# Attention's sums of values written feature-major, with the values as weights

## The chip, the cores and the metric

One Trainium2 chip, one core of it. The metric is device microseconds of one execution of the whole program. The core has five engines that run side by side: TensorE (PE, with its weight loads shown as PEld), VectorE (DVE), ScalarE (ACT), GpSimd (POOL) and SyncE (SP). All data transfers of the parts that matter here are issued from SP's queue, in order.

## What is computed

Two layers of a hybrid trunk over 1024 latent tokens and 256 context tokens. The token mixer of each layer has a Hyena long convolution, an mLSTM and an attention; the part that changes is the attention. It has 6 query heads in two groups of 3, one key/value head for each group, head size 64. A latent token sees the keys within 128 positions, all 256 context keys and a sink:

```python
s_loc = where(mask, einsum(q, k_window) * scale, -1e30)
s_ctx = einsum(q, k_ctx) * scale
p = softmax(concatenate([s_loc, s_ctx, s_sink]))
out = einsum(p_window, v_window) + einsum(p_ctx, v_ctx)
```

A context token sees the context keys and the sink alone. In the second layer only latent tokens are asked for. The concatenated heads go through one output projection.

## The kernel before

Everything is tiled to 128 rows. The program is written as Python generators, one for each stream of work, and `weave` takes steps from them in given proportions; a planner with a simulated timeline then sets the order of instructions on each engine, and each engine runs its own list in order.

`mix_heads` has two stages of interest in each layer. In the first, the projections (`project_o`, `attention_inputs` of both groups), the mLSTM and `attend` of group 0 are woven together. In the second, two halves of the Hyena convolution (`hyena`, with `dft4` on VectorE), the mLSTM and `attend` of group 1 are. After it `mixed` loads the heads' outputs back (`mixed_parts`) and runs the output projection.

`attention_inputs` normalises and rotates queries and keys, two token tiles at a time, transposes them, and puts the queries through the tile `qst` (one buffer) to the DRAM tensor `qd` with one store for two token tiles (L522).

`attend` runs over blocks of 128 queries: 10 blocks for each group in layer 0, 8 in layer 1, so 36 in all. `nk` is the number of 128-key tiles of a block: 5 for six of the eight latent blocks, 4 for the two at the ends, 2 for the two context blocks. For each of three heads:

- scores by matmuls in fp32r into the PSUM bank "s" (two buffers, L552 and L558), moved by VectorE into `S` (two buffers) with the running minimum, then exponentials with their sum on ScalarE (L561);
- `nk` transposes of `S` on TensorE into the bank "t" (L566; the fifth goes to a part of `po`, L570), copied by ScalarE into `PT` (two buffers, L567 and L571);
- `nk` matmuls in f32 that sum the values into `po`, the transposed weights being the stationary operand and 64 columns of `va` the moving one (L573):

```python
for i, kb in enumerate(kbs):
    nc.tensor.matmul(out=po[:, h * HD:(h + 1) * HD], lhsT=PT[:, i * P:(i + 1) * P], rhs=va[:, kb, :],
                     start=(i == 0), stop=(i == nk - 1))
```

After the third head the sums' reciprocals `es` are made. Here queries lie on the partitions, so three ScalarE instructions scale the heads (L148), two transposes turn the result (L585, L586), two ScalarE copies take it out of PSUM to `aev` (L589, L590), and two stores of 128 and of 64 partitions put it into the DRAM tensor `mixa` (L591, L592), laid out as 128 x 3 x tokens.

`split` (L136, L141) makes the fp32r halves of what `mixed_parts` loads (L1151).

Of the kernel before, what the change touches and what calls it, by code (L numbers as in the profile page):

```python
# [46 lines left out]
ON_PE = False  # L47
TK, TV, FW = (3, 2), (8, 7), (6, 1)
UW = 5, 3, 18
PT2 = 1  # L50
SC = (1, 0, 0, 1)
SB = ("f0", "f1"), ("t", "o")
WE, ML = (10, 10), (8, 8)
# [29 lines left out]
class Kernel:  # L83
# [388 lines left out]
    def attention_inputs(self, l, g, D, ap, ai):  # L472

        nc, A, d = self.nc, self.A, self.L[l]
        last = l == DEPTH - 1
        kt = self.t(ap, [P, T], F32R, "kk")
        va = self.t(ap, [P, NT, HD], F32, "va")
        qd = self.dram([P, 3, T], f"qd{g}")
        self.att[g] = (qd, kt, va)
        w = self.wgroup(l, f"g{g}")  # L480
        for t0 in (8, 6, 4, 2, 0):
            n = self.t(ai, [P, 2, 4, HD], F32, "n", bufs=2)
            for i in range(2):
                ps = self.tok_tile(w, t0 + i, 320)
                nc.scalar.activation(out=n[:, i], in_=ps[:, :256].rearrange("p (h d) -> p h d", h=4), func=AF.Copy)
                nc.scalar.activation(out=va[:, t0 + i, :], in_=ps[:, 256:320], func=AF.Copy)
                yield
            n3 = n.rearrange("p t h d -> p (t h) d")
            t1 = self.t(ai, [P, 8, HD], F32, "t1")
            nc.scalar.activation(out=t1, in_=n3, func=AF.Square)  # L490
            ss = self.t(ai, [P, 8], F32, "ss", bufs=2)
            nc.vector.tensor_reduce(out=ss, in_=t1, axis=AX.X, op=ALU.add)
            r = self.rsqrt(ai, ss, 1.0 / HD, [P, 8], "ar", 1)
            nc.vector.tensor_tensor(out=n3, in0=n3, in1=r.unsqueeze(2).to_broadcast([P, 8, HD]), op=ALU.mult)
            nc.gpsimd.tensor_tensor(out=n[:, :, 0:3], in0=n[:, :, 0:3], in1=d["qkw"][:, 0:1].unsqueeze(1).to_broadcast([P, 2, 3, HD]), op=ALU.mult)
            nc.gpsimd.tensor_tensor(out=n[:, :, 3], in0=n[:, :, 3], in1=d["qkw"][:, 1:2].to_broadcast([P, 2, HD]), op=ALU.mult)
            if t0 < 8:
                rt = self.t(ai, [P, 2, 2, HD], F32, "rt")
                nc.sync.dma_start(out=rt, in_=A["rope"][:, t0:t0 + 2])
                t2 = self.t(ai, [P, 8, HD], F32, "t1")  # L500
                for i in range(2):
                    t5 = t2[:, 4 * i:4 * i + 4].rearrange("p h (a b i) -> p h a b i", a=2, b=2)
                    n5 = n[:, i].rearrange("p h (a b i) -> p h a b i", a=2, b=2)
                    s5 = rt[:, i, 1, :].rearrange("p (a b i) -> p a b i", a=2, b=2)
                    for b in range(2):
                        nc.vector.tensor_tensor(out=t5[:, :, :, b, :], in0=n5[:, :, :, 1 - b, :],
                                                in1=s5[:, :, b, :].unsqueeze(1).to_broadcast([P, 4, 2, 16]), op=ALU.mult)
                    nc.gpsimd.tensor_tensor(out=n[:, i], in0=n[:, i], in1=rt[:, i, 0:1, :].to_broadcast([P, 4, HD]), op=ALU.mult)
                nc.vector.tensor_tensor(out=n3, in0=n3, in1=t2, op=ALU.add)
            hl = self.t(ai, [P, 2, 4, 2, HD], F32R, "hl")  # L510
            hf = hl.bitcast(F32)
            nc.scalar.activation(out=hl[:, :, :, 0, :], in_=n, func=AF.Copy)
            nc.vector.tensor_tensor(out=hl[:, :, :, 1, :], in0=n, in1=hf[:, :, :, 0, :], op=ALU.subtract)
            qst = self.t(ai, [P, 3, 2, P], F32, "qst")
            for i in range(2):
                tt = t0 + i
                pq = self.ps("f1")
                for h in range(4):
                    nc.tensor.transpose(pq[:, h * P:(h + 1) * P], hf[:, i, h].rearrange("p b d -> p (b d)"), self.ident)
                nc.scalar.activation(out=qst[:, :, i, :], in_=pq[:, :384].rearrange("p (h c) -> p h c", h=3), func=AF.Copy)  # L520
                nc.vector.tensor_copy(out=kt[:, tt * P:(tt + 1) * P], in_=pq[:, 384:])
            nc.sync.dma_start(out=qd[:, :, t0 * P:(t0 + 2) * P], in_=qst.rearrange("p h t c -> p h (t c)"))  # L522
            yield

    def attend(self, l, g, mix, ap):
        nc, d = self.nc, self.L[l]
        qd, kt, va = self.att[g]
        for nb in ORDER if l < DEPTH - 1 else ORDER[2:]:
# [8 lines left out]
            for i in range(2):  # L537
                for b in range(2):
                    nc.sync.dma_start(out=qf[b * HD:(b + 1) * HD, i], in_=qd[i * HD:(i + 1) * HD, :, nb * P:(nb + 1) * P])
            att = self.t(ap, [P, 3, HD], F32, "att", bufs=1)  # L540
            m3 = self.t(ap, [P, 3], F32, "m3", bufs=2)
            s3 = self.t(ap, [P, 3], F32, "s3", bufs=2)
            po = self.ps("o")
            for h in range(3):
# [14 lines left out]
                nc.vector.tensor_tensor_reduce(out=S[:, w:w + 256], in0=p2[:, :256], in1=self.amask[:, 384:640], scale=-0.125,  # L559
                                               scalar=init, op0=ALU.add, op1=ALU.min, accum_out=m3[:, h:h + 1])  # L560
                nc.scalar.activation(out=S[:, :w + 256], in_=S[:, :w + 256], func=AF.Exp, scale=-1.0, bias=m3[:, h:h + 1], accum_out=s3[:, h:h + 1])  # L561
                PT = self.t(ap, [P, 640], F32, "PT", bufs=2)
                pt1 = self.ps("t")
                n1 = min(nk, 4)
                for i in range(n1):
                    nc.tensor.transpose(pt1[:, i * P:(i + 1) * P], S[:, i * P:(i + 1) * P], self.ident)  # L566
                nc.scalar.activation(out=PT[:, :n1 * P], in_=pt1[:, :n1 * P], func=AF.Copy)  # L567
                if nk > 4:
                    pt2 = po[:, (2 + h % 2) * P:(3 + h % 2) * P]
                    nc.tensor.transpose(pt2, S[:, 4 * P:5 * P], self.ident)  # L570
                    (nc.scalar.copy if PT2 else nc.vector.tensor_copy)(out=PT[:, 4 * P:5 * P], in_=pt2)  # L571
                for i, kb in enumerate(kbs):
                    nc.tensor.matmul(out=po[:, h * HD:(h + 1) * HD], lhsT=PT[:, i * P:(i + 1) * P], rhs=va[:, kb, :],  # L573
                                     start=(i == 0), stop=(i == nk - 1))
                yield
            es = self.t(ap, [P, 3], F32, "es", bufs=2)
            nc.vector.tensor_tensor(out=es, in0=d["sink"][:, g * 3:g * 3 + 3], in1=m3, op=ALU.add)
            nc.scalar.activation(out=es, in_=es, func=AF.Exp)
            nc.vector.tensor_tensor(out=es, in0=es, in1=s3, op=ALU.add)
            nc.vector.reciprocal(out=es, in_=es)  # L580
            self.scale(att, po[:, :192].rearrange("p (h e) -> p h e", h=3), es, SC[0])
            af = att.rearrange("p h e -> p (h e)")
            pt = po[:, 2 * P:]
            big, small = (0, 128) if g == 0 else (64, 0)
            nc.tensor.transpose(pt[:, :P], af[:, big:big + P], self.ident)  # L585
            nc.tensor.transpose(pt[0:HD, P:2 * P], af[:, small:small + HD], self.ident)  # L586
            ev = self.t(ap, [P, 2, P], F32, "aev", bufs=1)
            cs = slice(nb * P, (nb + 1) * P)
            nc.scalar.activation(out=ev[:, 0, :], in_=pt[:, :P], func=AF.Copy)  # L589
            nc.scalar.activation(out=ev[0:HD, 1, :], in_=pt[0:HD, P:2 * P], func=AF.Copy)  # L590
            nc.sync.dma_start(out=mix["att"][:, 2 * g, cs], in_=ev[:, 0, :])  # L591
            nc.sync.dma_start(out=mix["att"][g * HD:(g + 1) * HD, 1, cs], in_=ev[0:HD, 1, :])  # L592
            yield


# [536 lines left out]
    def mixed_parts(self, mix, c, ops, late, room=()):  # L1132

        nc, (c0, n) = self.nc, c
        s = slice(c0, c0 + n)
        for ks in ((0, 1), (2,), (3, 4), (5,), (6, 7)) if late else ((0, 1), (2,), (6, 7), (3, 4), (5,)):
            if not room:
                raws = self.t(self.wp, [P, 1024], F32, "raw", 2)
            for i, k in enumerate(ks):
                raw = room[k].bitcast(F32)[:, :n] if room else raws[:, i * 512:i * 512 + n]  # L1140
                hi, lo = ops[k]
                if 3 <= k < 6:

                    R, b0 = (2, SEQ) if c0 >= SEQ else (8, 0)
                    j0, nj = (c0 - b0) // R, n // R
                    src = mix["hy"][:, k - 3, b0:b0 + P * R].rearrange("p (r j) -> p r j", r=R)[:, :, j0:j0 + nj]
                    ins = nc.sync.dma_start(out=raw.rearrange("p (r j) -> p r j", r=R), in_=src)
                    raw = raw.rearrange("p (r j) -> p j r", r=R)
                    hi, lo = (t.rearrange("p (j r) -> p j r", r=R) for t in (hi, lo))
                else:  # L1150
                    ins = nc.sync.dma_start(out=raw, in_=mix["att"][:, k, s] if k < 3 else mix["ml"][:, k - 6, s])  # L1151
                if "m" in TOK:
                    self.tc.stamp_issue_order_token(ins.ins, "loads")
                self.split(hi, lo, raw)
            yield
# [230 lines left out]
    def run(self):  # L1386
        with ExitStack() as st:
# [7 lines left out]
            hg = self.start()  # L1395
            xd = self.A["xin"]
            for l in range(DEPTH):
                mix = {"att": self.dram([P, 3, T], "mixa"), "hy": self.dram([P, 3, T], "mixh"), "ml": self.dram([P, 2, T], "mixm")}
                D = self.D
                self.project(l, D)  # L1400
                self.mix_heads(l, D, mix, hg)
# [430 lines left out]
```

## Time and profile before

| | us |
|---|---|
| median of 3 runs | 3440.06 |
| lowest and highest | 3439.55, 3443.77 |
| the profiled execution's own time | 3429.16 |
| its span, first to last instruction | 3427.4 |
| TensorE busy in it | 3195.6 (93%) |
| mean granted TensorE clock | 0.959 |

The profile is of one execution, which was faster than the median by 10.9 us; 1.8 us of its own time lie around the span. A row of a group gives busy time in all, mean time of one instruction in ns, and the engine's idle time ahead of the group with what ended it. A matmul's end is modelled, and matmuls overlap, so the time that one takes of the engine is read from the starts of its neighbours in the order of time, not from its mean. An f32 matmul that isn't a transpose shows as two records.

### The profile page before, as it was taken

How to read it: one execution, taken by the hardware profiler on the slowest of the kernel's cores; microseconds unless marked ns; L12 is line 12 of the kernel's file. 1: busy time of each engine (PE TensorE's matmuls, PEld its weight loads, DVE VectorE, ACT ScalarE, POOL GpSimd, SP SyncE). 2: the span in 40 equal slices, each digit the busy share in tenths (PEclk: the TensorE clock that was granted, in tenths of full speed). 3: DMA queues.
4: the chain of work that ended last, by engine and by line, in shares of the span. 5: the costliest groups of instructions: out<-in, count | busy, mean ns of one | idle time of the engine just before them, and what ended most of it. 6: DMA issues, size and time to landing. Idle time of an engine off the chain costs nothing. (4 is left out here: it accounts for less than half of the span.)

```text
span 3427.4 us, 48440 instructions
## 1 busy us (share of the span) xinstructions
PE 3195.6 (93%) x17486; PEld 2748.8 (80%) x17486; DVE 2072.1 (60%) x3673; ACT 1378.1 (40%) x2941; POOL 1071.9 (31%) x944
## 2 busy tenths in 40 slices
PE   7988999999979999997989999999889699999998
PEld 3966798888858888886867897899888478887787
DVE  8669667796494444344565755556885854444443
ACT  5544456444362223223451543456344533333210
POOL 2355333111142333334881230133112444433000
PEclk8999999999989999999999999999899899999999
DMA  6556545543611212126662364445336222223432
GB/s 236 194 196 210 172 138 170 142 120 91 185 57 59 74 68 74 59 74 237 227 230 87 118 203 152 148 134 179 102 90 194 68 74 80 80 83 104 157 98 74
DMA packets 336926, 449.09 MB, mean 131 GB/s; under 512 B 46576, under 2 KB 249124, under 8 KB 334895
## 3 DMA queue, kind: packets, MB, share of 16 engines
q1 hardware_dynamic: 336312, 445.67, 40.3%
q8 instruction: 138, 2.26, 0.3%
q14 instruction: 101, 0.83, 0.1%
q10 hardware_dynamic: 375, 0.34, 0.0%
HBM read 329.73 MB, written 116.16 MB: 130 GB/s over the span
## 5 line engine op out<-in xcount | busy, mean ns | idle before, releaser
L136 ACT ACTIVATE w<-raw 128x512 fp32r<-128x512 f32 (+3 forms) x286 | 221.1, 800 | 470.4 <-PE f L169 130.6
L168 PE MATMUL f<-b,w 128*128 128x512 f32 (+1 forms) x912 | 339.0, 383 | 49.2 <-ACT b L136 41.3
L141 DVE TENSOR_TENSOR w<-raw,w 128x512 fp32r<-128x512 f32 (+3 forms) x266 | 274.1, 1046 | 149.4 <-ACT w L136 141.5
L141 DVE TENSOR_TENSOR w<-S,w 128x512 fp32r<-128x512 f32 x168 | 145.7, 888 | 342.9 <-ACT w L136 322.7
L169 PE MATMUL f<-b,w 128*128 128x512 f32 (+1 forms) x912 | 334.8, 368 | 2.4 <-DVE b L141 2.4
L170 PE MATMUL f<-b,w 128*128 128x512 f32 (+1 forms) x912 | 333.3, 366 | 0.0
L168 PE MATMUL mm<-w,hh 128*128 128x256 f32 (+2 forms) x928 | 279.4, 302 | 8.3 <-ACT hh L326 5.4
L254 POOL TENSOR_TENSOR mraw<-mraw,silb 128x1024 f32<-128x1024 f32 x96 | 248.3, 2592 | 105.7 <-DVE mod L263 65.2
L170 PE MATMUL mm<-w,hl 128*128 128x256 f32 (+2 forms) x928 | 276.3, 300 | 4.8 <-DVE hl L327 4.8
L169 PE MATMUL mm<-w,hh 128*128 128x256 f32 (+2 forms) x928 | 278.1, 300 | 0.0
L1373 DVE SCALAR_TENSOR_TENSOR x<-f,mod,x 128x512 f32<-128x512 f32 (+1 forms) x256 | 166.3, 663 | 154.3 <-PE f L170 149.4
L168 PEld LDWEIGHTS f<-b,w 128*128 128x128 f32 x912 | 179.0, 199 | 86.5 <-ACT b L136 45.4
L169 PEld LDWEIGHTS f<-b,w 128*128 128x128 f32 x912 | 176.4, 193 | 32.4 <-DVE b L141 4.6
L170 PEld LDWEIGHTS f<-b,w 128*128 128x128 f32 x912 | 176.0, 193 | 26.9
L136 ACT ACTIVATE w<-S 128x512 fp32r<-128x512 f32 x168 | 101.0, 625 | 219.9 <-POOL S L1178 201.4
L168 PEld LDWEIGHTS mm<-w,hh 128*128 128x128 f32 x928 | 178.3, 192 | 12.9 <-ACT hh L326 7.4
L170 PEld LDWEIGHTS mm<-w,hl 128*128 128x128 f32 x928 | 177.4, 192 | 6.4 <-DVE hl L327 6.0
L169 PEld LDWEIGHTS mm<-w,hh 128*128 128x128 f32 x928 | 178.5, 192 | 0.8 <-DVE w L141 0.3
L271 ACT ACTIVATE mraw<-mraw 128x1024 f32<-128x1024 f32 x96 | 101.6, 1059 | 145.4 <-POOL mraw L254 145.4
L1240 PE MATMUL a<-hb,w 128*128 128x512 f32 x352 | 139.6, 397 | 7.9 <-DVE hb L141 7.8
L1240 PE MATMUL b<-hb,w 128*128 128x512 f32 x352 | 138.7, 394 | 8.2 <-DVE hb L141 8.0
L1239 PE MATMUL d<-hb,w 128*128 128x512 f32 x352 | 141.2, 401 | 4.5 <-ACT w L136 4.5
(678 smaller groups left out, 8893.3 us busy)
## 6 DMA issues: line engine op xcount, KB each, us to landing
mraw<-in_wmodT SPq DMA_DIRECT2D x96, 512.0 KB
raw<-in_wgu SPq DMA_DIRECT2D x88, 512.0 KB
act<-g SPq DMA_DIRECT2D x88, 256.0 KB
raw<-in_wdn SPq DMA_DIRECT2D x44, 512.0 KB
raw<-act SPq DMA_DIRECT2D x42, 512.0 KB
raw<-in_wout SPq DMA_DIRECT2D x32, 512.0 KB
q<-qd SPq DMA_DIRECT2D x144, 96.0 KB
eoL<-eo SPq DMA_DIRECT2D x64, 192.0 KB
```

The costliest lines, as they stand in the source:

```text
L136: ins = nc.scalar.activation(out=hi, in_=src, func=AF.Copy)
L141: (eng or nc.vector).tensor_tensor(out=lo, in0=src, in1=hi.bitcast(F32), op=ALU.subtract)
L168: nc.tensor.matmul(out=ps, lhsT=ah, rhs=bh, start=(i == 0), stop=False, skip_group_check=on)
L169: nc.tensor.matmul(out=ps, lhsT=ah, rhs=bl, start=False, stop=False, skip_group_check=on)
L170: nc.tensor.matmul(out=ps, lhsT=al, rhs=bh, start=False, stop=(i % part == part - 1 or i == n - 1), skip_group_check=on)
L254: nc.gpsimd.tensor_tensor(out=raw, in0=raw, in1=sil[v], op=ALU.mult)
L271: self.nc.scalar.activation(out=raw, in_=raw, func=AF.Copy, accum_out=o)
L1239: nc.tensor.matmul(out=ps, lhsT=ah[:, ks], rhs=bh, start=start and k == 0, stop=False, skip_group_check=not start)
L1240: nc.tensor.matmul(out=ps, lhsT=ah[:, ks], rhs=bl, start=False, stop=False, skip_group_check=not start)
L1373: nc.vector.scalar_tensor_tensor(out=x, in0=ps[:, :n], scalar=d["mod"][:, 40 + m, v:v + 1], in1=x, op0=ALU.mult, op1=ALU.add)
```

## The change

Values become the weights. For each key tile one matmul with `va[:, kb, :]` (128 x 64) as the stationary operand streams the transposed weights of all three heads, 384 columns, into `po[0:64]`; the result has features on partitions and queries along the row. `PT` becomes one tile for a whole block, 5 x 3 x 128 columns, with one buffer. The reciprocals, which lie on the query partitions, are spread over 64 partitions by a matmul of ones with `R`, three scaled identities side by side (made by ScalarE in a buffer of `S`), into a buffer of "s"; ScalarE copies the spread factors to `ev`, which lies in the last fifth of `PT`, and VectorE multiplies `po` by them. The scaling on L148, the two transposes and the two copies are gone. One store puts the 64 x 3 x 128 result into `mixa`, now laid out as 64 x 6 x tokens, and `mixed_parts` reads a 128-row tile of it with two loads of 64 partitions. `qst` holds one token tile, with a store for each.

```diff
-            qst = self.t(ai, [P, 3, 2, P], F32, "qst")
             for i in range(2):
                 tt = t0 + i
                 pq = self.ps("f1")
                 for h in range(4):
                     nc.tensor.transpose(pq[:, h * P:(h + 1) * P], hf[:, i, h].rearrange("p b d -> p (b d)"), self.ident)
-                nc.scalar.activation(out=qst[:, :, i, :], in_=pq[:, :384].rearrange("p (h c) -> p h c", h=3), func=AF.Copy)
+                qst = self.t(ai, [P, 3, P], F32, "qst")
+                nc.scalar.activation(out=qst, in_=pq[:, :384].rearrange("p (h c) -> p h c", h=3), func=AF.Copy)
                 nc.vector.tensor_copy(out=kt[:, tt * P:(tt + 1) * P], in_=pq[:, 384:])
-            nc.sync.dma_start(out=qd[:, :, t0 * P:(t0 + 2) * P], in_=qst.rearrange("p h t c -> p h (t c)"))
+                nc.sync.dma_start(out=qd[:, :, tt * P:(tt + 1) * P], in_=qst)
...
-            att = self.t(ap, [P, 3, HD], F32, "att", bufs=1)
+            PT = self.t(ap, [P, 5, 3, P], F32, "PT", bufs=1)
...
-                PT = self.t(ap, [P, 640], F32, "PT", bufs=2)
...
-                nc.scalar.activation(out=PT[:, :n1 * P], in_=pt1[:, :n1 * P], func=AF.Copy)
+                nc.scalar.activation(out=PT[:, :n1, h, :], in_=pt1[:, :n1 * P].rearrange("p (k c) -> p k c", k=n1), func=AF.Copy)
                 if nk > 4:
-                    pt2 = po[:, (2 + h % 2) * P:(3 + h % 2) * P]
-                    nc.tensor.transpose(pt2, S[:, 4 * P:5 * P], self.ident)
-                    (nc.scalar.copy if PT2 else nc.vector.tensor_copy)(out=PT[:, 4 * P:5 * P], in_=pt2)
-                for i, kb in enumerate(kbs):
-                    nc.tensor.matmul(out=po[:, h * HD:(h + 1) * HD], lhsT=PT[:, i * P:(i + 1) * P], rhs=va[:, kb, :],
-                                     start=(i == 0), stop=(i == nk - 1))
+                    nc.tensor.transpose(po[:, 3 * P:], S[:, 4 * P:5 * P], self.ident)
+                    nc.scalar.copy(out=PT[:, 4, h, :], in_=po[:, 3 * P:])
...
-            self.scale(att, po[:, :192].rearrange("p (h e) -> p h e", h=3), es, SC[0])
-            af = att.rearrange("p h e -> p (h e)")
-            pt = po[:, 2 * P:]
-            big, small = (0, 128) if g == 0 else (64, 0)
-            nc.tensor.transpose(pt[:, :P], af[:, big:big + P], self.ident)
-            nc.tensor.transpose(pt[0:HD, P:2 * P], af[:, small:small + HD], self.ident)
-            ev = self.t(ap, [P, 2, P], F32, "aev", bufs=1)
-            cs = slice(nb * P, (nb + 1) * P)
-            nc.scalar.activation(out=ev[:, 0, :], in_=pt[:, :P], func=AF.Copy)
-            nc.scalar.activation(out=ev[0:HD, 1, :], in_=pt[0:HD, P:2 * P], func=AF.Copy)
-            nc.sync.dma_start(out=mix["att"][:, 2 * g, cs], in_=ev[:, 0, :])
-            nc.sync.dma_start(out=mix["att"][g * HD:(g + 1) * HD, 1, cs], in_=ev[0:HD, 1, :])
+            R = self.t(ap, [P, 640], F32, "S", bufs=2)[:, :3 * P]
+            for h in range(3):
+                nc.scalar.activation(out=R[:, h * P:(h + 1) * P], in_=self.ident, func=AF.Copy, scale=es[:, h:h + 1])
+            for i, kb in enumerate(kbs):
+                nc.tensor.matmul(out=po[0:HD, :3 * P], lhsT=va[:, kb, :], rhs=PT[:, i].rearrange("p h c -> p (h c)"),
+                                 start=(i == 0), stop=(i == nk - 1))
+            pb = self.ps("s")
+            nc.tensor.matmul(out=pb[0:HD, :3 * P], lhsT=self.ones[:, 0:HD], rhs=R, start=True, stop=True)
+            ev = PT[0:HD, 4].rearrange("p h c -> p (h c)")
+            nc.scalar.activation(out=ev, in_=pb[0:HD, :3 * P], func=AF.Copy)
+            nc.vector.tensor_tensor(out=ev, in0=po[0:HD, :3 * P], in1=ev, op=ALU.mult)
+            nc.sync.dma_start(out=mix["att"][:, 3 * g:3 * g + 3, nb * P:(nb + 1) * P], in_=ev.rearrange("p (h c) -> p h c", h=3))
...
+                elif k < 3:
+                    for h in range(2):
+                        ins = nc.sync.dma_start(out=raw[h * HD:(h + 1) * HD], in_=mix["att"][:, 2 * k + h, s])
+                        if "m" in TOK and not h:
+                            self.tc.stamp_issue_order_token(ins.ins, "loads")
                 else:
-                    ins = nc.sync.dma_start(out=raw, in_=mix["att"][:, k, s] if k < 3 else mix["ml"][:, k - 6, s])
+                    ins = nc.sync.dma_start(out=raw, in_=mix["ml"][:, k - 6, s])
...
-                mix = {"att": self.dram([P, 3, T], "mixa"), "hy": self.dram([P, 3, T], "mixh"), "ml": self.dram([P, 2, T], "mixm")}
+                mix = {"att": self.dram([HD, 6, T], "mixa"), "hy": self.dram([P, 3, T], "mixh"), "ml": self.dram([P, 2, T], "mixm")}
```

## Rows read from the trace of the kernel before

**Rows 1.** The page's first part: busy time of each engine over the span.

```profile
...
PE 3195.6 (93%) x17486; PEld 2748.8 (80%) x17486; DVE 2072.1 (60%) x3673; ACT 1378.1 (40%) x2941; POOL 1071.9 (31%) x944
...
```

**Rows 2.** Stages around attention, layer 0 then layer 1: busy us, clock, DMA.

```profile
...
core 0: us, PE busy (x) PEld busy (x) DVE busy (x) ACT busy (x) POOL busy (x), PEclk, DMA share, GB/s
445.00:605.00 160.00, 154.89 (x1183) 148.68 (x1184) 102.48 (x350) 103.21 (x318) 55.37 (x66) 0.97 0.50 152
605.00:835.00 230.00, 210.15 (x1383) 198.41 (x1382) 189.07 (x438) 100.12 (x307) 29.48 (x35) 0.96 0.41 116
...
2255.00:2385.00 130.00, 125.58 (x937) 121.55 (x936) 74.41 (x260) 79.99 (x232) 40.56 (x49) 0.96 0.49 156
2385.00:2595.00 210.00, 186.75 (x1172) 176.47 (x1171) 171.29 (x387) 89.30 (x268) 33.02 (x34) 0.87 0.35 98
...
```

**Rows 3.** The same columns in slices of 40 us, layer 0.

```profile
...
480.00:520.00 40.00, 40.00 (x311) 39.33 (x310) 15.99 (x53) 23.19 (x68) 7.63 (x9) 1.00 0.30 94
...
680.00:720.00 40.00, 39.37 (x273) 38.52 (x273) 39.75 (x74) 14.65 (x46) 5.93 (x4) 1.00 0.35 104
...
```

**Rows 4.** Groups of instructions on TensorE by line and shape.

```profile
...
L573 PE MATMUL o<-va,PT 128*128 128x64 f32 x960 | 130.0, 285 | 8.6 <-ACT PT L571 7.7 <-ACT PT L567 0.7
...
L585 PE MATMUL o<-ident,att 128*128 128x128 f32 x36 | 10.5, 291 | 2.4 <-ACT att L148 2.3
L586 PE MATMUL o<-ident,att 128*64 128x128 f32 x36 | 10.1, 281 | 0.0
...
```

**Rows 5.** TensorE in order of time, layer 0, inside the first stage.

```profile
...
491.02 0.28 PE L169 MATMUL mm<-w,hh 128*128 128x256 f32 x1
491.14 0.27 PE L585 MATMUL o<-ident,att 128*128 128x128 f32 x1
...
491.28 0.36 PE L170 MATMUL mm<-w,hl 128*128 128x256 f32 x1
491.48 0.40 PE L558 MATMUL s<-kk,q 128*128 128x256 f32 x2
...
501.37 1.22 PE L573 MATMUL o<-va,PT 128*128 128x64 f32 x10
502.43 0.28 PE L570 MATMUL o<-ident,S 128*128 128x128 f32 x1
...
```

**Rows 6.** TensorE in order of time where 384 f32 columns stream.

```profile
...
202.94 0.81 PE L965 MATMUL f<-er,mfL 128*128 128x384 f32 x2
203.29 0.69 PE L169 MATMUL mm<-hl,w 128*128 128x512 f32 x1
203.82 0.40 PE L170 MATMUL mm<-hh,w 128*128 128x512 f32 x1
204.05 0.39 PE L168 MATMUL mm<-hh,w 128*128 128x512 f32 x1
...
```

**Rows 7.** Groups of instructions on ScalarE by line and shape.

```profile
...
L801 ACT ACTIVATE E<-E,gcols 128x128 f32<-128x128 f32 x144 | 46.2, 392 | 52.6 <-POOL E L799 52.4
...
L148 ACT ACTIVATE att<-o,es 128x64 f32<-128x64 f32 x108 | 25.8, 311 | 16.2 <-PE o L573 13.1 <-DVE es L580 2.9
...
L520 ACT ACTIVATE qst<-f 128x384 f32<-128x384 f32 x40 | 19.5, 487 | 13.7 <-PE f L519 13.7
...
L589 ACT ACTIVATE aev<-o 128x128 f32<-128x128 f32 x36 | 9.9, 275 | 9.9 <-PE o L586 8.5 <-DMA q<-qd 1.3
...
```

**Rows 8.** Groups of instructions on VectorE by line and shape.

```profile
...
L1102 DVE TENSOR_TENSOR Y<-h,hx 128x384 f32<-128x384 f32 x18 | 9.8, 548 | 3.8 <-PE h L1083 3.7
...
```

**Rows 9.** Chain that ended last, layer 1, first stage.

```profile
...
2259.82 3.61 DMA do<-ev
...
```

**Rows 10.** Waits of ScalarE, layer 0.

```profile
...
ACT ev L428 <- DMA do<-ev: 6.9, 7, 1.3
...
```

**Rows 11.** The tensor mixa: its stores, its loads, who waited for it.

```profile
...
L592 SPq DMA_DIRECT2D mixa<-aev x36: 451/483/1679, 469.1 to 2593.9; - x36
...
  ACT hb L136: 14.3, 6
...
```

More of the change, by code (lines that the diff above doesn't have):

```diff
@@ L49 @@
 UW = 5, 3, 18
-PT2 = 1
 SC = (1, 0, 0, 1)
```

## The prediction

> **What bounds the kernel now.** I read the page's first part, then the windows by stage, then TensorE's order of time inside a stage. The page says that TensorE is busy 93% of the span and VectorE 60% [rows 1], which is a mean over unlike stages. Attention runs in two of them in each layer. In the first, with the projections, TensorE is busy 154.9 of 160 us in layer 0 and 125.6 of 130 in layer 1 [rows 2], and there is a slice of 40 us in which it is busy all 40 at a granted clock of 1.00 [rows 3]: what is added to TensorE there comes out as time. In the second, with the Hyena convolution, TensorE is busy 91% and 89%, VectorE 82% and 82% [rows 2]; in the slice from 680 us on VectorE is at 39.75 of 40 and TensorE at 39.37 [rows 3]. Two engines take turns there as the bound. ScalarE is at 64% and 62% in the first stages and 44% and 43% in the second.
>
> **TensorE, step by step.** The sums of values are 960 records [rows 4], two for each f32 matmul. Ten of them start at 501.37 and the next instruction at 502.43 [rows 5], so a record takes 0.106 us, although only 64 columns stream. All cost 960 x 0.106 = 102 us. Afterwards each matmul covers three heads: 320 records of 384 columns. The trace has such a stream elsewhere: a pair of f32 records of 384 columns starts at 202.94, and with one 512-column matmul behind it holds the engine until 203.82; that matmul alone takes 0.23 (203.82 to 204.05) [rows 6]. So a pair costs 0.88 - 0.23 = 0.65 us, and 160 pairs cost 104 us. Six times the columns for a third of the records: a draw, +2 us. That the weights are 64 wide instead of 128 buys nothing in this sum: two transposes that differ only in that width have means of 291 and 281 ns [rows 4].
>
> New is the spreading matmul, one pair of 384 columns a block: 36 x 0.65 = +23.4. Gone are the two transposes of the scaled result: they start at 491.14, and with one 256-column matmul behind them they hold the engine until 491.48; the 256-column matmul ahead of them took 0.12 (491.02 to 491.14) [rows 5]. That leaves 0.22 a block, -7.9 in all. The sum for TensorE is +2 + 23 - 8 = **+17 us**, 0.49 a block.
>
> The bounds of it: if every wait for `PT` ahead of these matmuls went away too (8.6 us, and 2.4 ahead of the first transpose [rows 4]), +17 falls to +6. If the sums cost 0.60 a pair (a bare 3/4 of the pair's modelled 0.81 [rows 6]), they gain 6 instead of losing 2, and the sum is -2.
>
> **VectorE.** Added is one product of 64 x 384 with an operand in PSUM, a block. The same shape on 128 partitions takes 548 ns [rows 8]: 36 x 0.55 = +20 us. Nothing leaves this engine. In the first stage it has slack (102 of 160 us); in the second it counts.
>
> **ScalarE.** Gone are three scalings of 311 ns and two copies of 275 ns or less, 1.48 a block. Added are three scaled identities; the nearest row with a per-partition operand and 128 columns is 392 ns; and a copy of 384 columns out of PSUM at 487 ns [rows 7]: 1.66. The four identical copies into `PT` stay. A difference of 0.2 us a block, 7 us in all on an engine with a third or more idle: nothing.
>
> **Waits that the change adds.** Two tiles are now reused behind a store. `PT` has one buffer and ends as the source of the block's store, so the next block's first copy into it, on ScalarE, waits until that store has landed. `qst` is rewritten within one step, so the second tile's copy waits for the first's store. The trace has the like: `project_o` has one buffer `ev` in the first stage; its store takes 3.61 us from issue to release [rows 9], yet ScalarE waited for it only 6.9 us in 7 waits, 1.3 the longest [rows 10], as the planner puts other work ahead. Below: nothing. Above: 3.6 us for each of 20 second tiles and 36 blocks, 200 us of ScalarE, which can't all reach the end. With 1 us a wait, the row's mean, it is 56 us of ScalarE time, some of it with TensorE waiting behind for evictions. Queued behind a waiting copy on ScalarE are evictions of the projections' banks in the first stage and of the Hyena's bank in the second. I take 2 us for the end. Two smaller couplings (`R` takes a turn of `S`, the spread factors a turn of "s") hold the next block's scores until this block's tail; with 8 or 10 blocks in a stage of 130 us or more [rows 2], nothing.
>
> **SP's queue.** 36 stores of about 0.48 us issue go [rows 11], 20 of `qd` and 18 loads of `mixa` come: even. The loads are of 64 partitions each. ScalarE waited 14.3 us for such loads in 6 waits [rows 11], so slower ones could show: from 0 to +14, and I take 0, since `attend` goes from the last tokens to the first and the output projection begins with the last ones.
> The Trainium skill ("SBUF — State Buffer", section on the DMA port swizzle) says that 64 partitions reach only half of the memory's ports, so that one transfer of them gets half the bandwidth. By that rule the loads would be late and the sum would rise towards its upper bound by the 14 us; no row here shows a 64-partition load.
>
> **The sum.** First stages: 18 blocks x 0.49 = 8.8 us on a full TensorE. Second stages: 18 blocks, of which each adds 0.49 to TensorE and 0.55 to VectorE; either is idle a tenth to a fifth of the time, so I take half of the larger, 18 x 0.55 / 2 = 5.0. Waits: 2. Together +15.8 on the profiled 3429, which is the same on the median: 3440 + 14 to 16, **3455 us**. The profiled execution was 10.9 us below the median; I put the sum on the median.
>
> **Rivals.**
> 1. ScalarE stalls on the single-buffered `PT` and `qst`, and TensorE with it. For it: the chain runs through exactly such a store in the first stage [rows 9]. Against it: the short waits [rows 10]. If 0.5 us of each of the 56 new waits reaches the end, +28 on top: about 3483. It decides from some 1.8 us a wait on, half of a store's time. 10%.
> 2. Faster: the granted clock. It was 0.97, 0.96, 0.96 and 0.87 in the four stages [rows 2], which between the two levels (1.2 and 2.4 GHz) means that full speed was missing for 0.03 x 160 + 0.04 x 230 + 0.04 x 130 + 0.13 x 210 = 46 us of work. The drops lie where TensorE waited. Sums in one run of 10 records a block instead of three short runs, each behind a copy, leave fewer such places. If 60% came back, -28 + 16 = -12: 3428. It makes up for the added work from a third on (16 of 46) and decides from half on (23). Against it: most idle time in the second stage comes from VectorE, which gets more work. The two lower bounds for TensorE together, 17 - 11 - 19 = -13, would end there too. 21%.
> 3. Hidden: the second stage's idle time takes up all of its part, and the sums' waits pay for the first's. 3440 to 3446. 20%.
> 4. Late loads of `mixa`, the forecast and +14: 3469. 5%. By the Trainium skill's page named above this is what would happen; it has no row for it here, hence the small chance.
>
> **How the numbers follow.** The forecast has 44%, the rivals 10, 21, 20 and 5. A measurement of this kernel tells about 0.2%, 6.9 us, from no change. Faster by more than that: rival 2, 21%. Within it: rival 3 and a little of the forecast's low end, 21%. Slower: 58%. The range goes from 3431, which leaves out the better half of rival 2, to 3481, which leaves out most of rival 1; for the slower cases alone it would be 3447 to 3483.
>
> **What would show it.** Right: 320 records of 384 columns starting 0.32 us apart, 72 more for the spreading, TensorE's work in the first stages up by some 0.5 us a block at an unchanged clock, 36 VectorE products of 0.55, both stages longer by 4 to 5 us in each layer at most. Wrong: records of 384 columns much under 0.3 us apart; ScalarE waiting on stores out of `PT` or `qst` for more than 1 us each with TensorE idle; a granted clock near 1.00 in the second stages, above all in layer 1; or the planner's new order shifting the stages' ends by more than the sum, which no row of before can price.

## The result and the profile after

The changed kernel takes 3501.84 us (median of 4 runs, 3499.05 to 3510.77) against 3439.81 for the kernel before: ratio 1.0183, 95% interval 1.017 to 1.0196. It is slower, as forecast, but by 62 us where 15 were forecast, and outside the range (3431 to 3481). The profiled execution of it took 3500.81 us, with a span of 3499.0.

The page's first part, to be read beside [rows 1]:

```profile
span 3499.0 us, 47228 instructions
...
PE 3227.0 (92%) x16846; PEld 2674.7 (76%) x16846; DVE 2086.9 (60%) x3709; ACT 1386.2 (40%) x2905; POOL 1085.0 (31%) x944
...
```

TensorE is busy 31 us more (3227.0 against 3195.6), the span is 72 us longer (the medians differ by 62, since the profiled execution of before lies under its median). So more than half of these 72 us is no added busy time of TensorE. To see where it lies, the next view cuts out of each layer the stretch from the first block of attention to the last matmul of the output projection. It is the view of windows: the window, its length, the busy time of each engine, then TensorE's clock. First the kernel before:

```profile
...
440.00:973.70 533.70, 498.99 (x3422) 467.22 (x3421) 378.93 (x955) 264.12 (x748) 121.06 (x126) 0.96 0.47 139
2243.70:2688.70 445.00, 415.88 (x2630) 384.64 (x2629) 311.40 (x780) 213.28 (x583) 102.47 (x106) 0.93 0.46 139
sum 978.70, PE 914.88 PEld 851.86 DVE 690.33 ACT 477.40 POOL 223.53; mean PE 457.44 PEld 425.93 DVE 345.17 ACT 238.70 POOL 111.76
...
```

The changed kernel, same stretches:

```profile
...
440.00:1007.00 567.00, 515.70 (x3088) 431.62 (x3087) 386.23 (x977) 271.99 (x728) 126.45 (x127) 0.96 0.45 130
2282.10:2763.20 481.10, 430.32 (x2330) 346.71 (x2331) 321.99 (x807) 221.74 (x581) 109.39 (x106) 0.94 0.43 129
sum 1048.10, PE 946.02 PEld 778.33 DVE 708.21 ACT 493.73 POOL 235.84; mean PE 473.01 PEld 389.17 DVE 354.11 ACT 246.86 POOL 117.92
...
```

The two stretches grow by 69.4 us, nearly all of the 72. TensorE's busy time grows by 31.1, its idle time from 978.7 - 914.9 = 63.8 to 102.1, by 38.3. VectorE gains 17.9 (20 were forecast), ScalarE 16. The granted clock is level (0.96 and 0.93, then 0.96 and 0.94). Two questions follow: what the 38 us of idle time are, and whether the 31 are the forecast's 17.

The groups by line and shape answer to [rows 4], [rows 7] and [rows 8]:

```profile
...
L580 PE MATMUL o<-PT,va 128*64 128x384 f32 x320 | 118.2, 517 | 7.6 <-ACT PT L568 6.4 <-ACT PT L565 1.2
...
L564 PE MATMUL t<-ident,S 128*128 128x128 f32 x408 | 69.2, 293 | 26.2 <-ACT PT L565 16.2 <-ACT S L560 9.8
...
L578 ACT ACTIVATE S<-ident,es 128x128 f32<-128x128 f32 x108 | 36.1, 395 | 19.9 <-DVE es L574 16.2 <-DVE den L770 3.5
...
L583 PE MATMUL s<-S,ones 128*64 128x384 f32 x72 | 33.4, 549 | 3.3 <-ACT S L578 3.2
...
L586 DVE TENSOR_TENSOR PT<-o,PT 64x384 f32<-64x384 f32 x36 | 19.6, 545 | 24.8 <-PE o L580 17.8 <-ACT PT L585 5.8 <-ACT ev L429 1.0
...
L585 ACT ACTIVATE PT<-s 64x384 f32<-64x384 f32 x36 | 17.3, 481 | 72.2 <-PE o L580 44.1 <-PE s L583 28.0
...
```

The new instructions are as many as the prediction said and cost what it gave them: 320 records of 384 columns and 72 more, the product 545 ns (548 taken), a scaled identity 395 (392), the copy 481 (487). Not foreseen is the last row: ScalarE stood 72 us ahead of the copy of the spread factors, 44 of them until the sums were done.

Now one block's end in the changed kernel, layer 1 (timeline: start, duration, engine, line; in brackets idle time and what ended it):

```profile
...
2640.22 1.54 PE L583 MATMUL s<-S,ones 128*64 128x384 f32 x2
...
2641.69 1.01 PE L551 MATMUL s<-kk,q 128*128 128x384 f32 x2
...
2642.63 3.89 PE L580 MATMUL o<-PT,va 128*64 128x384 f32 x10
...
2644.42 0.14 PEld L580 LDWEIGHTS o<-PT,va 128*64 128x64 f32 x1 [0.18 <-issue]
2644.74 0.14 PEld L580 LDWEIGHTS o<-PT,va 128*64 128x64 f32 x1 [0.19 <-issue]
...
2646.55 0.48 ACT L585 ACTIVATE PT<-s 64x384 f32<-64x384 f32 x1 [0.77 <-PE o L580]
2646.89 0.30 PEld L557 LDWEIGHTS s<-kk,q 128*128 128x128 f32 x2
...
2648.01 0.47 DVE L558 CUSTOM_DVE_ANT_0 S<-s,amask,m 128x256 f32<-128x256 f32 x1
...
2648.52 0.83 ACT L560 ACTIVATE S<-S,m 128x640 f32<-128x640 f32 x1
...
```

The spreading (L583) takes one of the two buffers of "s". The next block's first scores (L551, 2641.69) get the other. Its second ones (L557) wait: for ten sums, and for the copy that empties the spread factors. They start at 2646.89, 5.2 us after the first ones, and the next block's first exp comes at 2648.52, after everything of this block. A record of the sums starts each 0.32 us, as predicted.

The same place in the kernel before:

```profile
...
2399.86 0.60 PE L552 MATMUL s<-kk,q 128*128 128x384 f32 x2
...
2404.70 0.61 DVE L553 CUSTOM_DVE_ANT_0 S<-s,amask,nsink 128x384 f32<-128x384 f32 x1
...
2405.67 0.72 ACT L148 ACTIVATE att<-o,es 128x64 f32<-128x64 f32 x3 [0.40 <-PE o L573]
...
2409.10 0.83 ACT L561 ACTIVATE S<-S,m 128x640 f32<-128x640 f32 x1
...
2409.51 0.27 PE L585 MATMUL o<-ident,att 128*128 128x128 f32 x1
...
2409.93 0.28 ACT L589 ACTIVATE aev<-o 128x128 f32<-128x128 f32 x1
...
```

The next block's first scores (L552) start at 2399.86, 9.7 us ahead of this block's transposes (L585), and its first exp at 2409.10 is ahead of them too. Two blocks overlap here; in the changed kernel they stand end to end.

A measure for this, used below as the **lag**: the time from the start of a block's reciprocals (L574, before: L580) to that of the next block's first exp, a mean over the blocks of a stage, in the order of the four stages. A large lag means that the two blocks stand end to end. Before: 2.1, 0.4, 2.4 and -0.9 us. Changed: 11.5, 13.1, 13.0 and 11.6.

What becomes late by it is the output projection, which needs all heads of a token tile. Its first matmul in layer 1, before and after:

```profile
...
2588.44 1.63 PE L1170 MATMUL p<-hb,w 128*128 128x512 f32 x3
...
2668.85 0.80 PE L1170 MATMUL p<-hb,w 128*128 128x512 f32 x1
...
```

Seen from the start of the stretch (2243.7 and 2282.1) it comes 42 us later. Attention's last store has moved from 2593.9 to 2677.6, behind that of the mLSTM, which ended last before (2649.5, now 2662.2). It is the same in layer 0: attention from 844.7 to 894.0, the mLSTM 865.6 and 866.4.

### The profile page after: what moved, and what is told of

The parts are those of the page before. It is cut to its first block, busy times and chain, and to the rows that moved or that the text cites. A ratio compares the mean times of both kernels' runs of the same rounds, so it can differ in the third digit from the quotient of the medians.

```text
span 3499.0 us, 47228 instructions
## 1 busy us (share of the span) xinstructions
PE 3227.0 (92%) x16846; PEld 2674.7 (76%) x16846; DVE 2086.9 (60%) x3709; ACT 1386.2 (40%) x2905; POOL 1085.0 (31%) x944
```

## The experiments

The theories that the expectations name. A, later S: blocks stand in line since a buffer is held to the block's end, by the spread factors' turn of "s" above all; P: also by `PT`, held until its store has landed. B, later T: the engines' added work. C: transfers of 64 partitions. R: the turn of `S` that `R` takes. The medians of the kernel before beside these runs were 3440.89 to 3444.65 us, and a ratio is to them. Each edit is one to the changed kernel, where not said otherwise. Every edit also makes the planner set a new order; the five edits to the kernel before other than f1 came out between 12 us under it and 3 over it, which gives an idea of how much a new order may move by itself.

**e5, another bank for the spread factors.**

```diff
-            pb = self.ps("s")
+            pb = self.ps("t")
```

> The change, but the spread factors go to the bank of the transposes instead of one of the two buffers of the scores. Theory A in a variant (the factors wait in a scores' buffer until the sums have read PT, so the next block's scores wait): 10 to 30 us come back. Theory A without the variant, B and C: within 7 us of 3502.

3462.54 us, ratio 1.0064 (1.0045 to 1.0082): 39 of the 62 us come back by this line, more than the 10 to 30 expected. The lag falls to 6.2, 6.6, 5.9 and 7.9. Windows of e5:

```profile
...
440.00:989.90 549.90, 513.50 (x3112) 433.73 (x3111) 393.59 (x985) 272.24 (x730) 129.70 (x128) 0.96 0.46 135
2261.90:2720.40 458.50, 422.00 (x2332) 345.98 (x2332) 323.11 (x805) 218.79 (x572) 114.84 (x107) 0.94 0.46 135
sum 1008.40, PE 935.50 PEld 779.70 DVE 716.70 ACT 491.03 POOL 244.54; mean PE 467.75 PEld 389.85 DVE 358.35 ACT 245.51 POOL 122.27
...
```

TensorE's idle time is 72.9, 9.1 over before; its busy time is 20.6 over before, near the forecast's 17. So 29 of the 38 us of idle time went with the turn, and 10 of the 31 of busy time. VectorE's waits for scores fall too. In the changed kernel (waits: total, times, longest):

```profile
...
DVE S L558 <- PE s L557: 36.0, 18, 5.4
...
DVE S L552 <- PE s L551: 34.3, 25, 4.2
...
```

and in e5:

```profile
...
DVE S L552 <- PE s L551: 26.6, 14, 4.0
...
DVE S L558 <- PE s L557: 10.5, 6, 3.9
...
```

70 us in the one, 37 in the other, 32 before. They don't measure the loss, though: they are 45 in f1 and 35 in e12, which are as slow as the changed kernel.

**f1 and f7, the turn alone, in the kernel before.** Its transposes of the scaled result go into a turn of "s" (f1), or of "t" (f7):

```diff
-            pt = po[:, 2 * P:]
+            pt = self.ps("s")[:, :2 * P]
```

> The kernel before with one edit: its two transposes of the scaled result go into a turn of bank "s" instead of the sums' own bank, so that a buffer of the scores is taken at the block's end and held until the result is copied out. Theory S: the coupling costs in the old kernel too, 3444 + 15 to 40, 3459 to 3484. If the price belongs to the three-head sums (PT complete only at the block's end), the old kernel with its sums spread over the block feels little: 3439 to 3452.

> The kernel before with its two transposes of the scaled result in a turn of bank "t" (one buffer, the transposes of the scores' exps), beside the run that put them into "s" and cost 72 us. Theory S (the price is how much of the next block stands behind the turn; behind "t" its scores and exps can go on): +5 to +20, 3448 to 3464. If any turn of a shared bank costs alike: 3490 or more.

f1: 3515.78 us, ratio 1.0211 (1.019 to 1.0232). 72 us, with no instruction added, where 15 to 40 were expected. f7: 3444.11, ratio 1.0012 (0.9998 to 1.0025), nothing clear of noise, where 5 to 20 were expected. Windows of f1:

```profile
...
440.00:1013.90 573.90, 526.36 (x3440) 491.19 (x3439) 379.68 (x963) 265.92 (x748) 125.87 (x127) 0.91 0.44 130
2288.90:2782.20 493.30, 437.99 (x2630) 401.00 (x2629) 316.25 (x792) 221.19 (x597) 100.75 (x106) 0.88 0.42 126
...
```

This execution lies 91 us over the profiled one of before. Idle time of TensorE: 1067.2 - 964.35 = 102.9, 39 over before, close to the changed kernel's 38. The rest is the clock: busy time times mean clock, an estimate of the work, is 526.4 x 0.91 + 438.0 x 0.88 = 864, and before 499.0 x 0.96 + 415.9 x 0.93 = 866, equal work, but 49 us longer at the lower clock. The lag is 12.0, 11.8, 14.6 and 10.8 in f1, and 2.6, 0.4, 2.4 and -0.6 in f7, as before. The bank "t" has one buffer and "s" two, and yet "t" costs nothing: behind "t" stand only the next block's transposes, behind "s" everything of it. f1's timeline shows it:

```profile
...
2454.88 1.33 PE L573 MATMUL o<-va,PT 128*128 128x64 f32 x10 [0.79 <-ACT PT L571]
...
2462.70 1.11 PE L566 MATMUL t<-ident,S 128*128 128x128 f32 x4 [3.03 <-ACT S L561]
...
2464.72 2.40 PE L573 MATMUL o<-va,PT 128*128 128x64 f32 x10 [0.69 <-ACT PT L571]
...
2476.92 0.16 DVE L580 RECIPROCAL es<-es 128x3 f32<-128x3 f32 x1
...
2477.75 0.48 PE L585 MATMUL s<-ident,att 128*128 128x128 f32 x1 [5.59 <-ACT att L148]
...
2477.88 0.78 PE L552 MATMUL s<-kk,q 128*128 128x256 f32 x2
...
```

The reciprocals come at 2476.92 (VectorE has other work between). Only behind the transposes of the result at 2477.75 the next block's first scores go, TensorE having waited 5.6 us. The ten sums at 2464.72 take 2.40 where those at 2454.88 took 1.33. The windows around them give the granted clock, the third number from the end:

```profile
...
2454.00:2457.00 3.00, 1.41 (x11) 1.19 (x10) 3.00 (x4) 0.75 (x2) 0.00 (x0) 1.00 1.01 310
...
2462.70:2465.00 2.30, 1.61 (x7) 1.21 (x7) 2.30 (x6) 0.75 (x2) 0.00 (x0) 0.50 0.00 0
...
```

TensorE went from the higher of its two levels to the lower between them, having stood idle for 2.2 us and 3.0 us.

**e18, a bank of another stream.** The spread factors go to "f0", the mLSTM's bank.

> The spread factors in bank "f0", which the mLSTM uses and attention does not: neither scores nor transposes of the next block wait for the turn, but the mLSTM's next product does. Theory S (what matters is that the next block's scores wait): the exps come early, and the time is at or under that with bank "t", 3448 to 3466. If any shared bank costs alike, 3480 or more.

3551.07 us, ratio 1.0307 (1.029 to 1.0325), 49 us over the changed kernel. The theory's range for this run was wrong by 85: the attention's lag does fall, to 4.6, 7.4, 5.6 and 6.1, but this bank, shared with another stream, cost more than one shared within attention. Both streams end later: in layer 0 the mLSTM's last store is at 907.8 us (changed kernel: 866.4) and attention's at 934.2 (894.0). How the two hold each other up was not followed further.

**e12, e9 and e13, what is held by the store.** e12 gives the result a tile of its own, so that `PT` is free with the sums; to make room the mLSTM's output weights are held in bf16. e13 adds e5's bank. e9 writes the result into `R`'s buffer instead.

```diff
-            ev = PT[0:HD, 4].rearrange("p h c -> p (h c)")
+            ev = self.t(ap, [P, 3 * P], F32, "aev", bufs=1)[0:HD]
```

> The changed kernel with the scaled result written to a tile of its own, so that PT comes free with the block's sums and no longer with the landing of its store (the mLSTM's output weights are held in bf16 to make room, which rounds them). The spread factors still take a turn of the scores' bank. Theory S (the turn of "s" alone makes the chain of a block long): the time stays near the changed kernel's 3502, 3494 to 3506. Theory P (PT's wait for the store is a second price): 10 to 25 us less, 3477 to 3492, and ScalarE's waits on DMA for PT gone.

> Both couplings taken away: spread factors in bank "t" and the result in a tile of its own (mLSTM output weights in bf16 again). Theory S alone: as with the bank alone, 3456 to 3469. Theory S and P: what is left is the added work of the engines, 3440 + 5 to 16, 3445 to 3456.

> The change, but the spread factors, the scaled result and the source of the store lie in R's buffer instead of the last fifth of PT, so PT is free when the sums are done. Theory A: the part of the chain from the sums' end to the store's landing (about 5 us of a block's 20) leaves PT's loop: 20 to 40 us come back, 3460 to 3480, less if the bank of the sums, which has one buffer too, holds the next block instead. Theories B and C: no change, 3500.

e12: 3500.64, ratio 1.0169 (1.0149 to 1.019), as the changed kernel. ScalarE no longer waits for `PT`'s store, nor ahead of the copy for the sums (44 us of the groups' last row), and no time comes back: theory P adds nothing to the 62. The lag stays as well, at 11.0, 11.8, 11.3 and 13.2, which points to the place of the turn in the line, and not to how long the copy stands in it. e13: 3470.47, 1.008 (1.0062 to 1.0097), not under e5. e9, where 20 to 40 us were expected back: 3511.99, 1.0204 (1.0189 to 1.0219), worse: now `S`, the buffer of the next block's scores, waits for the store (17.0 us of VectorE in 12 waits).

**e3 and e19, sums head by head** as before (128 columns, behind each head's transposes, `PT` with two buffers), e19 with e5's bank too. e3's core:

```diff
+                for i, kb in enumerate(kbs):
+                    nc.tensor.matmul(out=po[0:HD, h * P:(h + 1) * P], lhsT=va[:, kb, :], rhs=PT[:, i],
+                                     start=(i == 0), stop=(i == nk - 1))
```

> The change, but with the sums of values taken head by head again: values as weights, 128 columns streamed for each head as soon as its transposes are copied, PT a tile of one head with two buffers, the result and its store in a tile of their own. Theory A (the block's chain: one PT that is held from the first head's copy until the store has landed, and all sums put off to the block's end, make the attention stream late): most of the 62 us go, 3440 to 3460. Theory B (engine work: the spreading matmul and the product on VectorE): this work is unchanged, so about 3500 stays. Theory C (64-partition loads at the stages' ends): unchanged, about 3500.

> The changed kernel with its sums head by head, each right behind that head's transposes, through a PT of two buffers (480 matmuls of 128 columns instead of 160 of 384, the old cadence), and the spread factors in bank "t". If what is left comes from summing three heads at the block's end: 3441 to 3453. If not, 3456 to 3470, or more by the longer TensorE work of narrow matmuls.

e3: 3482.19, ratio 1.0115 (1.01 to 1.013). e19: 3479.69, 1.0109 (1.0094 to 1.0124). e3 misses both of its ranges: 20 us come back although the turn of "s" stays, and with it the lag (10.4 to 10.8). So sums head by head ease the price of that turn, why is not shown. They are not what is left over in e5: with its bank it is better to keep the three heads in one group.

**e14, e10, e16 and e17, the work and `R`.** e14 is e5 with the spreading in one pass (scaled identities and ones held as float32r). e10 leaves the scaling out altogether (no `R`, no spreading, no copy out of the bank; VectorE copies the sums). e16 is e5 with `R` in its own tile (bf16 weights as in e12); e17 is e14 and e16.

```diff
-            R = self.t(ap, [P, 640], F32, "S", bufs=2)[:, :3 * P]
+            R = self.t(ap, [P, 384], F32, "R", bufs=1)
```

> Spread factors in bank "t", and the spreading matmul in one pass (the scaled identities and the ones held as float32r, which rounds the factors): about 0.48 us less TensorE work a block, 17 us in all. Theory T (what is left of the slowdown, 18 us, is TensorE's added work, as the prediction's sum has it): 3441 to 3450. Theory R (it is the other coupling, R's turn of S): 3456 to 3467.

> The change without the division by the sum of exponentials: the three scaled identities, the spreading matmul, its copy on ScalarE are left out, and VectorE copies the sums to PT's last fifth instead of multiplying. The output is then not normalised. Theory B: the 23 us of TensorE work go, 3475 to 3480. Theory A: the chain from sums to store is shorter by about 2 us a block as well, 3450 to 3475. Theory C: 3500.

> Spread factors in bank "t", and R in a tile of its own instead of a turn of S (mLSTM output weights in bf16 to make room); the TensorE work stays. Theory R: the next block's first exp comes 2 to 3 us after the reciprocals, as before, instead of 6, and the time falls to 3444 to 3454. Theory T: the exps come earlier but the time stays, 3457 to 3470.

> The two edits together: spread factors in "t" by a matmul in one pass, R in a tile of its own. If both T and R hold 3435 to 3446, at or under the kernel before; if one of them, that one's range: 3441 to 3454; if neither, some 3460, and the rest lies in the order of the streams.

e14: 3458.38, ratio 1.0035 (1.0024 to 1.0047); e10: 3475.03, 1.0094 (1.0075 to 1.0113); e16: 3473.77, 1.0082 (1.0067 to 1.0098); e17: 3480.39, 1.0101 (1.0085 to 1.0117). Sums of the windows of e14:

```profile
...
sum 1009.60, PE 923.93 PEld 777.62 DVE 725.08 ACT 492.69 POOL 250.03; mean PE 461.96 PEld 388.81 DVE 362.54 ACT 246.34 POOL 125.01
...
```

and of e10:

```profile
...
sum 1014.20, PE 915.27 PEld 772.81 DVE 704.63 ACT 440.92 POOL 237.98; mean PE 457.63 PEld 386.41 DVE 352.31 ACT 220.46 POOL 118.99
...
```

e14 takes 11.6 us of busy time off e5, and 12.8 of idle time come in its place; e10 is at the busy time of before (915.3 and 914.9) and idle for 98.9. Work taken off TensorE here is not time, since something else is late next. In e10 it is the mLSTM. Attention's last store in layer 1 is back at 2596.7, but the mLSTM's comes at 2692.1, and the chain that ended last runs through it into the output projection:

```profile
...
2692.15 2.13 DMA mixm<-msq
...
2694.34 2.72 DMA hb<-mixm
...
2697.76 2.07 PE p L1164 x4
...
```

Another part shows in e16. Its lag is that of before (3.6, 0.3, 3.2, 0.0), so `R`'s turn is gone, and ScalarE now waits for `PT`'s store instead:

```profile
...
ACT PT L567 <- DMA mixa<-PT: 45.8, 22, 5.8
...
```

It is 18.2 us in e5, 39.8 in e10, and 3.1 in the changed kernel, where the scores were late anyway. It looks as if the couplings stood in series, one taking what another gives back; this is argued, not shown. Taking away `R`'s turn (e16) or the wait for the store (e13) came out 8 to 11 us over e5, and both e16 and e17 came out over all ranges of their expectations. A version with `R` and the result both apart was not run.

**e11, e7, f5, e8 and f6, the other parts alone.** e11 is e5 with `mixa` in the layout of before. The four others are edits to the kernel before: e7 the layout of 64 partitions, f5 `qst` a tile at a time, e8 one buffer of `PT`, f6 the bf16 weights as a control.

```diff
-            qst = self.t(ai, [P, 3, 2, P], F32, "qst")
...
+                qst = self.t(ai, [P, 3, P], F32, "qst")
...
+                nc.sync.dma_start(out=qd[:, :, tt * P:(tt + 1) * P], in_=qst)
```

> Spread factors in bank "t", and mixa in the layout of the kernel before: two stores of 64 partitions a block, and the output projection's loads of 128 partitions, half as many. Theory C (loads and stores of 64 partitions cost): 8 to 14 us under the bank's 3462, 3448 to 3456. Otherwise 3457 to 3468.

> The kernel before with another part alone: mixa with 64 partitions, that is three stores a block and loads of 64 partitions, twice as many. If loads of 64 partitions are late (the rival of late loads): 3450 to 3460. If not, 3440 to 3450, the third store's issue being some 0.6 us a block on SP.

> The kernel before with one part of the change: qst one buffer a tile, one store a tile (20 stores of qd instead of 10). If the single buffer behind its store is part of what is left (18 us): 3449 to 3462. If its waits are hidden: 3438 to 3449.

> The kernel before with one buffer of PT instead of two: a head's copy waits for the sums of the head ahead. The single buffer of PT is the last part of the change not tried by itself. If it is part of what is left: 3450 to 3460. If a single buffer is hidden, as qst's was: 3438 to 3449.

> A control: the kernel before with the mLSTM's output weights in bf16, the edit that made room in four of the runs. If it costs nothing 3438 to 3449; if the runs with it came out late because of it, 3449 to 3458.

e11: 3479.3, ratio 1.0105 (1.0089 to 1.0122), slower than e5 and over both of its ranges: it has two stores a block, and ScalarE's waits for `PT`'s stores are 27.1 us (18.2 in e5), so it does not test the loads alone. e7: 3439.55, 0.9998 (0.9987 to 1.001): ScalarE's waits for `mixa` rise from 10.6 us to 26.0, hidden. f6: 3446.0, 1.0004 (0.9994 to 1.0014), so the bf16 edit is free. Two parts gain a little, and why is not shown. e8: 3434.41, 0.9982 (0.997 to 0.9994). f5: 3430.66, 0.9968 (0.9954 to 0.9981), under both kernels, though its one buffer does wait:

```profile
...
ACT qst L520 <- DMA qd<-qst: 8.2, 3, 3.3
...
```

## Why the prediction was wrong, by its steps

**What failed** is the last sentence on waits: "Two smaller couplings (`R` takes a turn of `S`, the spread factors a turn of "s") hold the next block's scores until this block's tail; with 8 or 10 blocks in a stage of 130 us or more, nothing." The coupling was seen and priced at nothing; the turn of "s" is worth 39 us of the 62 (e5), and 72 in the kernel before (f1). The argument by the stage's length took it that a block's chain fits into its share of the stage, 16 us in the first stages. It fits there because two blocks overlap: from first exp to first exp it is 16.0 and 17.2 us in the first stages before, 19.6 and 22.7 after. And attention is now the last stream to end in both layers: in layer 1 its last store comes at 2677.6, 72 us behind the Hyena's last at 2605.2, where it was 13 us behind (2593.9 and 2580.5).

**TensorE's sum** was right in kind: cadence 0.32 as predicted, and in e5, where no turn of "s" disturbs, busy time rises by 20.6 us for the 17. But its price is not one to one. e14 took 11.6 us of it away and gained 4 us by the medians (10 by the ratios), and e10, with no added busy time, is slower than e5. That the added work comes out as the forecast's 9 us in the first stages and 5 in the second is shown by no run.

**VectorE's** 20 measured 19.6 for the new products and 17.9 for the engine; what they cost in time is not shown. **ScalarE's** "nothing" left out that the copy waits in its queue for the sums, as it writes into the fifth of `PT` that they read: 44 us of standing. By e12 that cost no time.

**Rival 1** (`PT` and `qst` behind their stores) is not what the 62 us are: e12 gains nothing, f5 and e8 put single buffers into the kernel before and cost nothing (in e8 `PT` waits for the sums, not for a store). The waits of `PT` become long only once the scores come early (e16).

**Rival 2** (clock): 0.96 and 0.94 over the stretches, level with before; no share came back. Its second support was added up wrongly: the lower bound for the sums is 8 us under the forecast's term, not 19, so the two bounds together give -2 and not -13, about 3438. **Rival 3** (hidden) is refuted by the result. **Rival 4** (late loads) is refuted by e7: ScalarE's waits rise by 15 us, close to the 14 of the rival, and the time stays. (The 14.3 us that it starts from were waits for loads of 128 partitions, not for "such loads".) That a load of 64 partitions gets half the bandwidth, which the prediction cites from the Trainium skill, "SBUF — State Buffer", section on the DMA port swizzle, is neither shown nor refuted here, as the last section tells.

**The last of its "wrong" signs**, an order that shifts the stages' ends by more than the sum, is nearest to what came.

**What stays open** are e5's 18 us by the medians (22 by the ratio), or 30 if f5's gain, whose edit e5 contains, holds there too. In the trace, where e5 and before lie 28 us apart, TensorE's added busy time (20.6) and idle time (9.1) add up to about that, but e14 and e10 show that it is not the work as such. The planner's new order is a rival for a part of these 18 us: the five small edits to the kernel before moved by up to 12, and no run held the order fixed. That the remaining couplings take turns in binding (`R` for `S`, `PT` for its store) is argued from e16's waits, and not shown by a run without them. What makes the mLSTM late in e10 is open as well.

## What to carry to other kernels

A buffer taken in turn has a place in line: ask of each new use what stands behind it, and how early that started before the change. The trace of before has the measure, how far the next block's first step lies ahead of this block's last one; an edit that takes this lead away costs the overlap, even where it adds no instruction (f1). Keeping the lead is not enough, for e10 and e16 have it and are some 30 us slower than before all the same. By these runs a short-lived product late in a block should take its turn in the bank whose next user comes latest ("t" here), and neither in that of the next block's first step nor in another stream's; and the parts of a change are worth timing one by one, since two of them gained a little while the whole lost.

## What was not expected of the hardware

In f1 the lost overlap was paid twice: it has 39 us more idle time and 49 us more busy time for the same work, at a mean clock of 0.91 and 0.88 instead of 0.96 and 0.93, while the changed kernel with 38 us more idle time stayed at 0.96 and 0.94. All five executions of f1 show it (0.946 to 0.948 over the span, 0.953 or more in each of the kernel before). Why the one lost clock and the other did not is open.

Whether a load of 64 partitions is slower by the byte can't be read from these runs, though two of them seem to say that it is not. In the changed kernel (issues: KB each, median us to landing):

```profile
...
hb<-mixa SPq DMA_DIRECT2D x18, 128.0 KB, 2.9
...
```

of 128 partitions in e11:

```profile
...
hb<-mixa SPq DMA_DIRECT2D x9, 256.0 KB, 5.6
...
```

and the first again in e5, which differs from e11 by the layout alone:

```profile
...
hb<-mixa SPq DMA_DIRECT2D x18, 128.0 KB, 4.6
...
```

Half the bytes take half the time against the first of these, and four fifths of it against the second. The same 128 KB land in 2.5 us in e16 and in 5.8 in e18, so the median moves with more than the layout.
